# Group norms whose sums of squares are taken two products of z later, in a fused decoder step

## The chip, the cores and the metric

The kernel runs on one core of a Trainium2 chip. The metric is the device time of one execution in microseconds (us); lower is better. The engines are named as the profile names them: PE (TensorE matmul), DVE (VectorE), ACT (ScalarE), POOL (GpSimd) and SP (SyncE, which only issues DMAs here).

## What is computed

One inference step of a two-layer decoder for 1024 new prompt tokens and 8 short sample sequences (1104 token columns in all): a layer with a Mamba-2 mixer and an MLP, and a layer with attention and an MLP. The change lies in the first layer's mixer, between the state-space scan and the residual stream. What the scan gives, y, is gated by z, normed in 8 groups of 256 features, and projected:

```python
def gated_group_rmsnorm(y, z, w):
    g = (y * jax.nn.silu(z)).astype(jnp.float32)
    shp = g.shape
    g = g.reshape(shp[:-1] + (N_GROUPS, shp[-1] // N_GROUPS))
    g = g * lax.rsqrt(jnp.mean(g * g, axis=-1, keepdims=True) + EPS)
    return (g.reshape(shp) * w.astype(jnp.float32)).astype(y.dtype)
...
    y, h_new = ssd_scan(xs, dt, a_neg, bm, cm, h0)
...
    out = gated_group_rmsnorm(y, z, gate_w) @ w_out
```

z is the part of the input projection, `rmsnorm(h) @ w_in`, with 2048 columns: 8 groups of 256.

## The kernel before

Everything is kept with features in partitions and tokens along the free axis. Every fp32 product is three matmuls of split operands (`mm3`, L204 to L206: high weight by high data, high by low, low by high).

**The scan.** `ssd` (L609) runs group by group, in each group first a step for the sample tokens (t = 8) and then eight steps of 128 tokens. The step for the samples multiplies the states h by their decay on POOL (L716, four times), adds the new part in four pieces on DVE (L725, each from a pair of matmuls L723 and L724), and forms outputs (L679, L688). The prompt's steps form the next state from a state product (L729) and an addition (L734).

**The gate groups.** `gate_group` (L739) does for one group and each of three chunks of tokens (384, 384, 336) two products of z, one per tile of 128 features, of 24 matmuls each. After each, ACT takes tanh (L753) and DVE forms silu (L754). Then POOL multiplies y in (L759), ACT squares (L760), DVE adds the two tiles (L761) and `rstd` gives the scale: `sum_over` splits the sum into a high part (ACT, L248, `msh`) and a low part (DVE, L249, `msl`), PE multiplies both by ones (L250, L253), and ACT takes Ln (L261) and Exp (L262), each with a load of its function table. DVE multiplies scale and weight into the result (L765, twice). At the end of groups 0 to 5 `side_sums` (L776) stores sums of blocks of the result to DRAM (`z_d`); groups 6 and 7 are stored as they are (`g_d`, L774). The buffer that holds silu and squares comes from a ring of two tiles (`n3`), so chunk c + 2 waits for the last use in chunk c.

The function is a generator. Group 0 is mixed into the scan's last group: the table in `mixer` tells how many of its steps are taken after which scan step. Groups 1 to 7 run back to back in `gates_out` (L799).

**The output product.** `block_products` (L1182) multiplies with a scheme of seven block products instead of eight, in two blocks b, four output tiles p, seven products i. A block product is 18 matmuls of 276 columns. Its operands are seven slots, each loaded from `z_d` (L1174) and split by ACT (L1178) and DVE (L1179): for b = 0 a tile `A5`, two in `R0`, and four pieces of the buffer `S` that held the normed input of the z products, so these four can be loaded only when the last z product is done. Their splits are made in `more`, after products 1 to 4 of the first output tile. The weights of an output tile p are two raw tiles (L1113), of which DVE forms sums (L1119, L1125) and ACT and POOL the split parts (L1000, L1001). Raw tiles of odd p are taken from the ring `n3` that the norm also uses. Results are added by DVE (L1213), the first copied by ACT (L1232). PE's result banks are named `ma` to `md`.

The order on each engine is set by a scheduler when the program is built: it takes the earliest instruction in program order that its own timeline has ready, so code order sets priority and not place. `keep_in_program_order` on an instruction (argument `pin` of `sum_over`) keeps it from being taken before what stands ahead of it.

Of the kernel before, what the change touches and what calls it, by code (L numbers as in the profile page):

```python
# [16 lines left out]
P = 128  # L17
# [124 lines left out]
class Kernel:  # L142
# [96 lines left out]
    def sum_over(self, ssum, n, pin=False):  # L239


        nc = self.nc
        if self.pstat is None:
            ms = self.gps()
        else:
            ms = self.pstat[0].tile([P, 512], F32, tag=self.pstat[1], bufs=self.pstat[2], name="ms")
# [492 lines left out]
    def gate_group(self, g, xs, y, gt, tmp):  # L739
# [6 lines left out]
        for c, (o, n) in enumerate(CH):  # L746
            yv = [t[:, o:o + n] for t in y]
            g2 = gt(c)[:, :, :n]
            for j in range(2):
                pt = self.gps()  # L750
                self.mm3(pt[:, :n], [(w[j][0][:, k], w[j][1][:, k]) for k in range(KT)],
                         [(xs[c][0][:, k, :n], xs[c][1][:, k, :n]) for k in range(KT)])
                nc.scalar.activation(out=g2[:, j], in_=pt[:, :n], func=AF.Tanh, scale=0.5)  # L753
                nc.vector.scalar_tensor_tensor(out=g2[:, j], in0=g2[:, j], scalar=1.0, in1=pt[:, :n],  # L754
                                               op0=ALU.add, op1=ALU.mult)
                yield
# [5 lines left out]
            rs = self.rstd(g2[:, 0], n, self.eps4, D / 256, g2[:, 1])  # L762
            for j in range(2):
                ft = 2 * g + j
                nc.vector.scalar_tensor_tensor(out=yv[j], in0=yv[j],  # L765
                                               scalar=self.nv[:, ft % 8, 6 + ft // 8:7 + ft // 8], in1=rs,
                                               op0=ALU.mult, op1=ALU.mult)
            yield
        if g < 2 * KB:
# [29 lines left out]
    def gates_out(self, xs, big, cr, co):  # L799
# [3 lines left out]
        self.more_banks(cr, 4)  # L803
# [10 lines left out]
        slots = [[A5] + B + S[:4], [S[4], None, A5] + S[:4]]  # L814
        load, parts = self.side_io(self.rz, slots)
        with ExitStack() as cy:
            yp = self.pool("yp", ctx=cy)
            for g in range(1, G):
                y = yp.tile([P, 2, T], F32, tag="y", bufs=2, name="gy")
                for _ in self.gate_group(g, xs, [y[:, 0], y[:, 1]], lambda c: self.n3(),  # L820
                                         lambda: yp.tile([P, nn], F32, tag="m", bufs=2, name="gm")):
                    pass
                self.split_ahead()
                if g == 4:
                    for i in range(3):
                        load(0, i)
                if g in (5, 6):
                    for i in ((0,), (1, 2))[g - 5]:
                        parts(0, i)
# [3 lines left out]
        dp = self.pool("dp", ctx=co)  # L833
        us = dp.tile([P, 4, nn], F32, name="us")
        slots[1][1] = dp.tile(slot, F32R, name="A6")
# [296 lines left out]
    def down_blocks(self, layer, rd, rt, R0, big, c0, chs):  # L1132
# [12 lines left out]
        slots = [A, B + A[:5], A[5:] + B + A[:3], A[3:] + A[:3]]  # L1145
# [24 lines left out]
    def side_io(self, rt, slots):  # L1170
        nc = self.nc

        def load(b, i):
            nc.sync.dma_start(out=slots[b][i][:, 1].bitcast(F32), in_=rt[b][:, i // 2, i % 2])  # L1174

        def parts(b, i):
            x = slots[b][i]
            nc.scalar.copy(out=x[:, 0], in_=x[:, 1].bitcast(F32))  # L1178
            nc.vector.tensor_tensor(out=x[:, 1], in0=x[:, 1].bitcast(F32), in1=x[:, 0].bitcast(F32), op=ALU.subtract)  # L1179
        return load, parts  # L1180

    def block_products(self, w, big, us, slots, load, parts, free, make, last, more, early=(0, 0)):  # L1182
# [31 lines left out]
        for b in range(nb):  # L1214
            for p in range(4):
# [3 lines left out]
                for i, (wh, wl) in enumerate(self.down_weights(w[b], p)):  # L1219
# [4 lines left out]
                    x = slots[b][i]  # L1224
                    for k in range(2):
                        cs = slice(k * qw, k * qw + qw)
                        self.mm3(banks[e][:, 512 + (k - 1) * qw:512 + k * qw], [(wh[:, q], wl[:, q]) for q in range(KB)],
                                 [(x[:, 0, q, cs], x[:, 1, q, cs]) for q in range(KB)], new)
# [503 lines left out]
    def first_layer(self, cb):  # L1732
# [6 lines left out]
        with ExitStack() as ch:  # L1739
            cr = ExitStack()  # L1740
            self.banks(cr, 3)
            with ExitStack() as cm:
                self.fmp = self.pool("fmp", ctx=cm, right=True)
                self.cw = self.pool("cw", ctx=cm, right=True)
                with ExitStack() as c1:
                    xs = self.mixer(c1)
            big = self.pool("hp", ctx=ch, right=True).tile([P, KT, T], F32, name="hh")
            hts = [big[:, :, o:o + n] for o, n in CH]
            done, norm = self.entry(big, h_d, self.ncol(2))
            with ExitStack() as self.cR:  # L1750
                with ExitStack() as co:
                    self.gates_out(xs, big, cr, co)
# [94 lines left out]
    def mixer(self, c1):  # L1847
# [36 lines left out]
        for g in range(G):  # L1884
# [7 lines left out]
            for t in self.ssd(g, fm):  # L1892
                for k in range({8: 3, 2: 1, 3: 1, 4: 1, 6: 1, 7: 1}.get(t, 0) if gate is not None else 0):
# [75 lines left out]
```

## Time and profile before

| | |
|---|---|
| runs shown, us | 2946.33, 2947.52, 2948.03 (median 2947.52) |
| the profiled execution, us | 2948.11 |
| its span in the trace, us | 2946.4 |
| mean granted clock of PE | 0.985 |
| busy: PE, DVE, ACT, POOL | 96%, 64%, 49%, 47% |
| share of the chain that ended last: PE, DVE, issue, ACT, DMA, POOL | 72%, 9%, 6%, 5%, 5%, 4% |

The span is the stretch from the first to the last recorded instruction. A timeline row has the start in us, the length in us, the engine, the line and the operation, then result and operands, and in brackets the idle time of that engine ahead of it and what ended it. Starts of matmuls are a better guide than their lengths, since they are pipelined.

### The profile page before, as it was taken

What the parts mean: (1) busy time and instruction counts of PE and PEld (TensorE: products, weight loads), DVE (VectorE), ACT (ScalarE), POOL (GpSimd) and SP (SyncE); (2) the same over time, 40 slices, a digit from 0 to 9 for tenths busy, and PEclk for the clock granted to TensorE, in tenths of its full rate; (3) what the DMA queues carried; (4) which work ended last, traced back from release to release, by engine and by line L of the source; (5) the groups of instructions that cost most, each with busy time, mean ns of one, the idle gap of its engine ahead of it and who ended that gap; (6) DMA issues with size and microseconds to landing.
All of it is one profiled execution on the core that took longest, in us unless ns stands there. A gap on an engine that the chain in (4) does not pass through costs nothing.

```text
span 2946.4 us, 51820 instructions
## 1 busy us (share of the span) xinstructions
PE 2819.3 (96%) x19895; PEld 2710.3 (92%) x19895; DVE 1894.1 (64%) x3026; ACT 1454.8 (49%) x2781; POOL 1381.2 (47%) x1279
## 2 busy tenths in 40 slices
PE   8999999989878999999999999999999999999998
PEld 6999999978878999999999999988889999999997
DVE  6788777765546666454546766675678554367675
ACT  6555555556665355545433425555555545433333
POOL 5566666665445714444346663312112444345562
PEclk9999999999999999999999999999999999999999
DMA  3344444447554233444645522447454444543422
GB/s 136 95 125 128 123 122 124 129 136 268 186 196 142 87 113 117 151 140 150 245 159 190 183 80 69 160 155 266 143 177 171 140 147 135 203 151 123 144 99 76
DMA packets 219329, 433.46 MB, mean 147 GB/s; under 512 B 30713, under 2 KB 128377, under 8 KB 216505
## 3 DMA queue, kind: packets, MB, share of 16 engines
q1 hardware_dynamic: 219080, 430.14, 44.3%
q8 instruction: 157, 2.57, 0.4%
q14 instruction: 92, 0.75, 0.1%
HBM read 302.71 MB, written 128.32 MB: 146 GB/s over the span
## 4 chain that ended last, share of the span: by engine, by line
PE 72%; DVE 9%; issue 6%; ACT 5%; DMA 5%; POOL 4%; SPq 0%; DVEq 0%; POOLq 0%; ACTq 0%
PE g L204 9%; PE g L205 9%; PE g L206 9%; PE mc L204 3%; PE mc L206 3%; PE mc L205 3%; PE ma L204 3%; PE ma L206 3%; PE ma L205 3%; PE md L205 2%; PE md L206 2%; PE mb L204 2%; PE mb L205 2%; PE mb L206 2%; PE md L204 2%
## 5 line engine op out<-in xcount | busy, mean ns | idle before, releaser
L1001 POOL TENSOR_TENSOR w<-s,w 128x384 fp32r<-128x384 f32 (+1 forms) x272 | 369.6, 1364 | 394.1 <-ACT w L1000 390.0
L204 PE MATMUL g<-S,w 128*128 128x384 f32 (+2 forms) x1584 | 536.0, 339 | 2.4 <-ACT w L170 0.8
L205 PE MATMUL g<-S,w 128*128 128x384 f32 (+2 forms) x1584 | 536.3, 339 | 0.0
L206 PE MATMUL g<-S,w 128*128 128x384 f32 (+2 forms) x1584 | 532.9, 337 | 3.5 <-POOL w L171 2.7
L1001 POOL TENSOR_TENSOR w<-raw,w 128x384 fp32r<-128x384 f32 (+1 forms) x204 | 263.7, 1298 | 283.6 <-ACT w L1000 250.5
L171 POOL TENSOR_TENSOR w<-raw,w 128x1024 fp32r<-128x1024 f32 x96 | 244.1, 2543 | 274.9 <-ACT w L170 201.9
L206 PEld LDWEIGHTS g<-S,w 128*128 128x128 f32 x1584 | 304.1, 192 | 5.4 <-POOL w L171 3.0
L204 PEld LDWEIGHTS g<-S,w 128*128 128x128 f32 x1584 | 303.1, 191 | 5.9 <-issue 1.8
L205 PEld LDWEIGHTS g<-S,w 128*128 128x128 f32 x1584 | 303.7, 192 | 1.0 <-issue 0.5
L1000 ACT CAST w<-s 128x384 fp32r<-128x384 f32 (+1 forms) x272 | 150.0, 557 | 298.5 <-DVE s L1125 70.8
L204 PE MATMUL ma<-S,w 128*128 128x276 f32 (+1 forms) x808 | 235.2, 291 | 8.2 <-DVE us L1213 6.7
L206 PE MATMUL ma<-S,w 128*128 128x276 f32 (+1 forms) x808 | 234.5, 290 | 0.0
L205 PE MATMUL ma<-S,w 128*128 128x276 f32 (+1 forms) x808 | 234.3, 290 | 0.0
L1000 ACT CAST w<-raw 128x384 fp32r<-128x384 f32 (+1 forms) x204 | 112.2, 556 | 166.3 <-PE mc L206 49.1
L593 DVE SCALAR_TENSOR_TENSOR fm<-xp,cv,fm 128x1024 f32<-128x1024 f32 x96 | 161.1, 1681 | 33.1 <-ACT fm L574 32.5
L204 PEld LDWEIGHTS ma<-S,w 128*128 128x128 f32 x808 | 153.2, 190 | 9.9 <-issue 5.6
L205 PE MATMUL g<-R,w 128*128 128x384 f32 (+2 forms) x480 | 158.1, 329 | 0.0
L206 PE MATMUL g<-R,w 128*128 128x384 f32 (+2 forms) x480 | 157.9, 329 | 0.0
L204 PE MATMUL g<-R,w 128*128 128x384 f32 (+2 forms) x480 | 157.7, 329 | 0.0
L205 PEld LDWEIGHTS ma<-S,w 128*128 128x128 f32 x808 | 153.5, 190 | 0.0
L206 PEld LDWEIGHTS ma<-S,w 128*128 128x128 f32 x808 | 153.3, 190 | 0.0
L204 PE MATMUL mc<-S,w 128*128 128x276 f32 (+1 forms) x512 | 148.4, 290 | 1.9 <-DVE hh L1213 1.9
(489 smaller groups left out, 8671.1 us busy)
## 6 DMA issues: line engine op xcount, KB each, us to landing
raw<-in_w_up_dram SPq DMA_DIRECT2D x64, 512.0 KB
raw<-in_w_in_dram SPq DMA_DIRECT2D x48, 512.0 KB
raw<-in_w_downs_dram SPq DMA_DIRECT2D x64, 384.0 KB
w<-ws_o SPq DMA_DIRECT2D x48, 512.0 KB
w<-ws_q SPq DMA_DIRECT2D x40, 512.0 KB
ab<-acs_d SPq DMA_DIRECT2D x64, 256.0 KB
S<-t_d SPq DMA_DIRECT2D x18, 828.0 KB
S<-t_e SPq DMA_DIRECT2D x18, 816.0 KB
```

Of the source, the lines that this page charges most:

```text
L171: nc.gpsimd.tensor_tensor(out=wl, in0=raw, in1=wh.bitcast(F32), op=ALU.subtract)
L204: mm(out=out, lhsT=wh, rhs=xh, start=(first and k == 0), stop=False)
L205: mm(out=out, lhsT=wh, rhs=xl, start=False, stop=False)
L206: mm(out=out, lhsT=wl, rhs=xh, start=False, stop=(k == n - 1))
L593: nc.vector.scalar_tensor_tensor(out=acc[:, :SEQ], in0=xp[:, k:k + SEQ], scalar=cv[:, j, k:k + 1], in1=acc[:, :SEQ], op0=ALU.mult, op1=ALU ...
L1000: nc.scalar.copy(out=t[:, 0], in_=src)
L1001: nc.gpsimd.tensor_tensor(out=t[:, 1], in0=src, in1=t[:, 0].bitcast(F32), op=ALU.subtract)
```

## The change

`gate_group` no longer ends a chunk with its norm. It gives control back twice per chunk instead of three times, and puts the norm (the new `gate_norm`) into a list with a count of 3; `tick`, called once per product of z, counts down and runs what is due, so a norm is written two products behind its chunk, with its first ones-matmul pinned. Group 0's table of steps has one entry less. Group 1 begins, with two chunks, before the next buffers are opened. The last two chunks' norms would have no products of z behind them: they are run from `more`, after the first output tile's products 3 and 6, with their sums in a bank of the output product. To let the last group's y live that long its pools are laid out anew: the two y tiles come from pools of their own, and the operand `A6` is made of a rest of `S` and of a y tile, so slots are lists of pieces.

```diff
@@ gate_group
                 nc.vector.scalar_tensor_tensor(out=g2[:, j], in0=g2[:, j], scalar=1.0, in1=pt[:, :n],
                                                op0=ALU.add, op1=ALU.mult)
-                yield
+                if j == 0:
+                    self.tick()
+                    yield
...
             nc.vector.tensor_tensor(out=g2[:, 0], in0=g2[:, 0], in1=g2[:, 1], op=ALU.add)
-            rs = self.rstd(g2[:, 0], n, self.eps4, D / 256, g2[:, 1])
-            for j in range(2):
-                ft = 2 * g + j
-                nc.vector.scalar_tensor_tensor(out=yv[j], in0=yv[j],
...
+            self.due.append([3, partial(self.gate_norm, g, c, y, g2, tmp)])
+            self.tick()
             yield
+
+    def tick(self, n=1):
+
+        for e in self.due:
+            e[0] -= n
+        while self.due and self.due[0][0] <= 0:
+            self.due.pop(0)[1]()
+
+    def gate_norm(self, g, c, y, g2, tmp):
+        nc = self.nc
+        o, n = CH[c]
+        rs = self.rstd(g2[:, 0], n, self.eps4, D / 256, g2[:, 1], pin=True)
+        for j in range(2):
+            ft = 2 * g + j
+            yv = y[j][:, o:o + n]
+            nc.vector.scalar_tensor_tensor(out=yv, in0=yv, scalar=self.nv[:, ft % 8, 6 + ft // 8:7 + ft // 8], in1=rs,
+                                           op0=ALU.mult, op1=ALU.mult)
+        if c < 2:
+            return
@@ gates_out
-        slots = [[A5] + B + S[:4], [S[4], None, A5] + S[:4]]
+        slots = [[[(t[:, 0], t[:, 1])] for t in ts] for ts in ([A5] + B + S[:4], [S[4], A5, A5] + S[:4])]
...
+        for g in range(1, G):
+            for _ in gate if g == 1 else self.gate_of(g, xs, yps):
+                pass
...
         def more(b, p, i):
-            if (b, p) == (0, 0) and 1 <= i <= 4:
+            if (b, p) != (0, 0):
+                return
+            if 1 <= i <= 4:
                 parts(0, i + 2)
+            if i in (3, 6):
+
+                self.pstat = (self.pq, self.CHAIN[0][3], 1, 1024)
+                self.tick(2 if i == 3 else 9)
+                self.pstat = None
+            if i == 6:
+
+                t = ya.tile([P, 4, nn], F32R, tag="y", bufs=1, name="A6")
+                rest = self.S.rearrange("p e k n -> p (e k n)")[:, 5 * size:].rearrange("p (q n) -> p q n", q=2)
+                slots[1][1] = [(rest, t[:, 0:2]), (t[:, 2:3], t[:, 3:4])]
...
-                            (lambda: self.block_load(rd, 3, R0), lambda j: self.block_parts(j, R0)), more, (0, 1))
+                            (lambda: self.block_load(rd, 3, R0), lambda j: self.block_parts(j, R0)), more, (1, 1))
@@ side_io, parts
-            x = slots[b][i]
-            nc.scalar.copy(out=x[:, 0], in_=x[:, 1].bitcast(F32))
-            nc.vector.tensor_tensor(out=x[:, 1], in0=x[:, 1].bitcast(F32), in1=x[:, 0].bitcast(F32), op=ALU.subtract)
+            for hi, lo in slots[b][i]:
+                nc.scalar.copy(out=hi, in_=lo.bitcast(F32))
+                nc.vector.tensor_tensor(out=lo, in0=lo.bitcast(F32), in1=hi.bitcast(F32), op=ALU.subtract)
@@ first_layer
+                gate = self.gate_of(1, xs, yps)
+                for _ in range(4):
+                    next(gate)
             big = self.pool("hp", ctx=ch, right=True).tile([P, KT, T], F32, name="hh")
@@ mixer
-                for k in range({8: 3, 2: 1, 3: 1, 4: 1, 6: 1, 7: 1}.get(t, 0) if gate is not None else 0):
+                for k in range({8: 2, 2: 1, 3: 1, 6: 1, 7: 1}.get(t, 0) if gate is not None else 0):
```

What this moves is shown at three places by the written order of the engines; the changed program has its own line numbers (a norm's multiplies are L783 there, L765 before; the h additions L726 and L725; ones-matmuls L251, L254 and L250, L253; operand casts L1212 and L1178; weight loads L1143 and L1113).

DVE in the scan's last group, from the first to the fourth addition to the states h, before:

```order
L725 TENSOR_TENSOR h_7085<-h_7085,st 128x512
L679 TENSOR_TENSOR yo<-y,ef 128x256
L765 SCALAR_TENSOR_TENSOR gy<-gy,nv,gt 128x384 x2
L688 SCALAR_TENSOR_TENSOR yt<-fm,dcol,y 128x128 x2
L632 TENSOR_TENSOR xdt<-tp,dt 128x256
L725 TENSOR_TENSOR h_7085<-h_7085,st 128x512
L649 TENSOR_TENSOR dec<-dec,cbm 128x512
L641 TENSOR_TENSOR cbm<-cb,tri 128x128
L725 TENSOR_TENSOR h_7085<-h_7085,st 128x512
```

and now:

```order
L726 TENSOR_TENSOR h_7085<-h_7085,st 128x512
L680 TENSOR_TENSOR yo<-y,ef 128x256
L689 SCALAR_TENSOR_TENSOR yt<-fm,dcol,y 128x128 x2
L633 TENSOR_TENSOR xdt<-tp,dt 128x256
L726 TENSOR_TENSOR h_7085<-h_7085,st 128x512
L650 TENSOR_TENSOR dec<-dec,cbm 128x512
L633 TENSOR_TENSOR xdt<-tp,dt 128x256
L642 TENSOR_TENSOR cbm<-cb,tri 128x128
L726 TENSOR_TENSOR h_7085<-h_7085,st 128x512
```

The two multiplies of group 0's first norm stood between the first and the second addition; now they stand 33 rows behind the second.

PE at the end of the last product of z, before (`ma<-A` is the output product's first):

```order
L206 MATMUL g<-S,w 128x336
L250 MATMUL ms<-msh,ones_r 128x384
L253 MATMUL ms<-msl,ones_r 128x384
L250 MATMUL ms<-msh,ones_r 128x336
L253 MATMUL ms<-msl,ones_r 128x336
L204 MATMUL ma<-A_7815,w 128x276
```

and now, at the same place and where the last sum went:

```order
L206 MATMUL g<-S,w 128x336
L251 MATMUL ms<-msh,ones_r 128x384
L254 MATMUL ms<-msl,ones_r 128x384
L204 MATMUL ma<-A_7967,w 128x276
...
L206 MATMUL md<-S,w 128x276
L251 MATMUL ms<-msh,ones_r 128x336
L254 MATMUL ms<-msl,ones_r 128x336
L205 MATMUL mc<-S,w 128x276
```

Chunk 1's sums stay in front of the output product; chunk 2's stand behind its first six products, ahead of all but one matmul of the seventh.

ACT behind the last product of z now, from chunk 1's Ln to chunk 2's high part (`n_9421` is chunk 1's buffer, `n_9492` chunk 2's):

```order
L262 ACT_TABLE_LOAD
L262 ACTIVATE n_9421<-ms,eps 128x384
L1030 CAST w<-raw 128x384 x2
L763 ACTIVATE n_9492<-gy 128x336
L1212 CAST S<-S 128x1656
L263 ACT_TABLE_LOAD
L263 ACTIVATE n_9421<-n_9421 128x384
L763 ACTIVATE n_9492<-gy 128x336
L1212 CAST S<-S 128x1656
L1266 COPY us<-ma 128x552
L1212 CAST S<-S 128x1656
L249 CAST msh<-n_9492 128x336
```

Two more casts of `S` follow, one cast of a weight sum and one of a raw weight, and then the Ln and Exp of chunk 2, each with its table load. Before, chunk 1's Ln and Exp stood ahead of the first cast, chunk 2's Ln and Exp among the last two.

## Rows read from the trace of the kernel before

**Rows 1.** Busy time by stage: stretch, length, busy us of PE, PEld, DVE, ACT, POOL, granted clock, DMA

```profile
606.00:635.05 29.05, 23.41 (x155) 20.09 (x154) 18.49 (x39) 16.38 (x39) 17.27 (x18) 0.88 0.38 94
635.05:668.00 32.95, 30.49 (x204) 26.64 (x205) 23.30 (x52) 18.88 (x43) 25.34 (x27) 1.00 0.64 199
668.00:876.00 208.00, 181.96 (x999) 175.46 (x998) 109.09 (x148) 136.35 (x197) 96.07 (x62) 0.95 0.58 206
876.00:892.25 16.25, 2.47 (x4) 1.31 (x5) 11.23 (x15) 11.90 (x17) 3.10 (x3) 0.56 0.66 267
895.01:905.90 10.89, 8.64 (x64) 7.97 (x63) 8.24 (x9) 7.41 (x11) 8.29 (x7) 1.00 0.46 149
905.90:917.20 11.30, 11.30 (x89) 11.30 (x90) 8.63 (x11) 4.45 (x7) 6.05 (x6) 1.00 0.79 274
```

**Rows 2.** What PE waited for, 668 to 870 us: total us, times, longest

```profile
PE ms L253 <- DVE msl L249: 14.8, 8, 3.0
PE ms L250 <- ACT msh L248: 9.6, 8, 2.6
```

**Rows 3.** Timeline of ACT, end of the scan

```profile
624.64 1.28 ACT L261 ACT_TABLE_LOAD   x1 [4.48 <-PE g L253]
```

**Rows 4.** Timeline of DVE, end of the scan: the additions to the states h

```profile
621.46 0.69 DVE L725 TENSOR_TENSOR h<-h,st 128x512 f32<-128x512 f32 x1 [1.40 <-POOL h L716]
...
630.30 0.68 DVE L725 TENSOR_TENSOR h<-h,st 128x512 f32<-128x512 f32 x1
...
634.22 0.68 DVE L725 TENSOR_TENSOR h<-h,st 128x512 f32<-128x512 f32 x1
```

**Rows 5.** Timeline of PE, the first prompt step's state product

```profile
635.05 0.67 PE L729 MATMUL st<-xd,Bt 128*128 128x256 f32 x2 [0.50 <-DVE h L725]
```

**Rows 6.** Timeline of POOL, the states' decay

```profile
616.30 5.12 POOL L716 TENSOR_TENSOR h<-h,eendb 128x512 f32<-128x512 f32 x4
```

**Rows 7.** Busy time of the block products' tile `ma` in two stretches, PE first

```profile
892.25:895.01 2.76, 2.76 (x12) 2.76 (x13) 0.00 (x0) 0.00 (x0) 0.50 0.00 0
906.97:909.26 2.29, 2.29 (x18) 2.23 (x18) 0.00 (x0) 0.00 (x0) 1.00 1.09 332
```

**Rows 8.** Timeline of PE, end of the gate groups and output product

```profile
880.00 0.69 PE L250 MATMUL ms<-msh,ones_r 128*128 128x384 f32 x1 [4.03 <-ACT msh L248]
881.26 0.69 PE L253 MATMUL ms<-msl,ones_r 128*128 128x384 f32 x1 [0.57 <-DVE msl L249]
890.09 0.65 PE L250 MATMUL ms<-msh,ones_r 128*128 128x336 f32 x1 [8.15 <-ACT msh L248]
891.80 0.65 PE L253 MATMUL ms<-msl,ones_r 128*128 128x336 f32 x1 [1.06 <-DVE msl L249]
...
917.06 0.29 PE L206 MATMUL mb<-R,w 128*128 128x276 f32 x1
```

**Rows 9.** Timeline of ACT, end of the gate groups

```profile
882.03 1.28 ACT L261 ACT_TABLE_LOAD   x1 [0.38 <-PE ms L253]
883.32 0.58 ACT L261 ACTIVATE n<-ms,eps 128x384 f32<-128x384 f32 x1
...
885.64 1.55 ACT L1178 CAST S<-S 128x1656 fp32r<-128x1656 f32 x1
...
889.57 0.47 ACT L248 CAST msh<-n 128x336 fp32r<-128x336 f32 x1 [0.52 <-DVE n L761]
```

**Rows 10.** Timeline of DVE, start of the output product

```profile
899.20 1.03 DVE L765 SCALAR_TENSOR_TENSOR gy<-gy,nv,n 128x336 f32<-128x336 f32 x2
900.16 1.87 DVE L1179 TENSOR_TENSOR S<-S 128x1656 fp32r<-128x1656 f32 x1
...
905.51 0.69 DVE L1119 TENSOR_TENSOR s<-raw 128x384 f32<-128x384 f32 x1 [2.00 <-DMA raw<-in_w_outs_dram]
```

**Rows 11.** DMA issues of SP, start of the output product

```profile
899.79 0.80 SPq L774 DMA_DIRECT2D g_d<-gy  x2
900.68 0.81 SPq L1113 DMA_DIRECT2D raw<-in_w_outs_dram  x1
```

More of the change, by code (lines that the diff above doesn't have):

```diff
@@ L245, in sum_over @@
         else:
[L246 removed]
+            ms = self.pstat[0].tile([P, self.pstat[3] if len(self.pstat) > 3 else 512], F32, tag=self.pstat[1],
+                                    bufs=self.pstat[2], name="ms")
         hi, lo = (self.np.tile([P, 384], F32R, tag="n1", bufs=5, name="ms" + p)[:, :n] for p in "hl")
@@ L797, in side_sums, with gate_of, gates_out @@
             nc.sync.dma_start(out=d[:, 2, 1, cs], in_=t)
-    def gates_out(self, xs, big, cr, co):
+    def gate_of(self, g, xs, yps):
+        y = yps[g % 2].tile([P, 2, T], F32, tag="y", bufs=1, name="gy")
+        return self.gate_group(g, xs, [y[:, 0], y[:, 1]], lambda c: self.n3(),
+                               lambda: yps[0].tile([P, T // 2], F32, tag="m", bufs=2, name="gm"))
+    def gates_out(self, xs, big, cr, co, cb, yps, gate):
         nc = self.nc
         nn = T // 2
-        self.more_banks(cr, 4)
+        ya = yps[1]
         for c, (o, n) in enumerate(CH):
@@ L813, in gates_out @@
         B = cut(R0.rearrange("p e k n -> p (e k n)"), 2)
-        slots = [[A5] + B + S[:4], [S[4], None, A5] + S[:4]]
+        slots = [[[(t[:, 0], t[:, 1])] for t in ts] for ts in ([A5] + B + S[:4], [S[4], A5, A5] + S[:4])]
         load, parts = self.side_io(self.rz, slots)
[L816 to L829, printed above, removed]
+        for g in range(1, G):
+            for _ in gate if g == 1 else self.gate_of(g, xs, yps):
+                pass
+            self.split_ahead()
+            if g == 4:
+                for i in range(3):
+                    load(0, i)
+            if g in (5, 6):
+                for i in ((0,), (1, 2))[g - 5]:
+                    parts(0, i)
         cr.close()
@@ L1144, in down_blocks @@
         B = cut(R0.rearrange("p e k n -> p (e k n)"), 2)
-        slots = [A, B + A[:5], A[5:] + B + A[:3], A[3:] + A[:3]]
+        slots = [[[(t[:, 0], t[:, 1])] for t in ts] for ts in (A, B + A[:5], A[5:] + B + A[:3], A[3:] + A[:3])]
         free = [(0, 1, 2, 3, 4), (0, 1, 2, 3, 4), (0, 1, 4, 5, 6)]
@@ L1173, in load @@
         def load(b, i):
-            nc.sync.dma_start(out=slots[b][i][:, 1].bitcast(F32), in_=rt[b][:, i // 2, i % 2])
+            q = 0
+            for hi, lo in slots[b][i]:
+                m = lo.shape[1]
+                nc.sync.dma_start(out=lo.bitcast(F32), in_=rt[b][:, i // 2, i % 2, q:q + m])
+                q += m
         def parts(b, i):
-            x = slots[b][i]
-            nc.scalar.copy(out=x[:, 0], in_=x[:, 1].bitcast(F32))
-            nc.vector.tensor_tensor(out=x[:, 1], in0=x[:, 1].bitcast(F32), in1=x[:, 0].bitcast(F32), op=ALU.subtract)
+            for hi, lo in slots[b][i]:
+                nc.scalar.copy(out=hi, in_=lo.bitcast(F32))
+                nc.vector.tensor_tensor(out=lo, in0=lo.bitcast(F32), in1=hi.bitcast(F32), op=ALU.subtract)
         return load, parts
@@ L1223, in block_products @@
                         banks[e] = self.pq.tile([P, 1024], F32, tag=e, bufs=1, name="m" + e)
-                    x = slots[b][i]
+                    x = [(hi[:, q], lo[:, q]) for hi, lo in slots[b][i] for q in range(lo.shape[1])]
                     for k in range(2):
@@ L1227, in block_products @@
                         self.mm3(banks[e][:, 512 + (k - 1) * qw:512 + k * qw], [(wh[:, q], wl[:, q]) for q in range(KB)],
-                                 [(x[:, 0, q, cs], x[:, 1, q, cs]) for q in range(KB)], new)
+                                 [(hi[:, cs], lo[:, cs]) for hi, lo in x], new)
                     pv = banks[e][:, 512 - qw:512 + qw]
@@ L1750, in first_layer @@
             with ExitStack() as self.cR:
-                with ExitStack() as co:
-                    self.gates_out(xs, big, cr, co)
+                with co:
+                    self.gates_out(xs, big, cr, co, cz, yps, gate)
                 self.out_last(hts, done, norm)
```

13 lines of the change are left out of this document (7 added, 6 removed).

## The prediction

> **What bounds the kernel now.** I read the busy shares first, then TensorE's (PE's) busy time stage by stage, then the list of what PE waited for, and last the timelines around the places that the change moves. PE is busy 96% of the span, so time can only be won where PE idles or runs at its lower clock (a granted clock of 0.50, 1.2 GHz, against 1.00, 2.4 GHz). The stage table [rows 1] shows that in the part that the change touches. In 606 to 635 us (end of the state-space scan, with gate group 0 mixed in) PE is busy 23.41 of 29.05 us at a mean granted clock of 0.88. In 668 to 876 (gate groups 1 to 7) it idles 26.0 us in 16 or more short waits. In 876 to 892.25 (the last group's norm) it works 2.47 of 16.25 us, and in 895 to 905.9 it idles 2.25 us more. After 905.9 it never idles. These are the three places: start, middle, end.
>
> **The middle: 0, bounds -2 and +2.** The waits there are all for the operands of the ones-matmuls that add up a group's squares: 14.8 us for the low part on VectorE (DVE), 9.6 us for the high part on ScalarE (ACT) [rows 2]. One reads the change as pushing these sums back behind two more products of z, which would remove all of it. But the written order of PE differs there by three matmuls at most in group 1 and not at all in groups 2 to 6: the scheduler had already put each sum some 40 to 90 matmuls (two to four products) behind the product that feeds it, and the pin fixes what was there. ACT's and DVE's orders agree as well. So the 24 us of waits stay; I allow 2 us either way for shifted buffers and transfers.
>
> **The start: -4.5, bounds -7.5 and +1.** Before, chunk 0's norm stands among the last scan steps. ACT reaches its Ln at 624.64, after waiting 4.48 us for PE's low sum [rows 3]; DVE's four additions to the state h stand around the two multiplies of that norm, and run from 621.46 to 634.90, the second only at 630.30 [rows 4]. The first state product of the prompt's steps then starts at 635.05, after a wait of 0.50 for the last h addition [rows 5]. In the change no norm stands between these additions (the order of DVE above), and the 24 z products that PE ran between the two sums come earlier, where it idled. How early can that state product be? By DVE: POOL's four multiplies on h run 616.30 to 621.42 [rows 6]; after them four additions of 0.69 with a matmul pair of some 0.7 between them take 4 x 0.69 + 4 x 0.7 = 5.6, so 627.5 to 628 if POOL starts them a little later. By PE's own work: 29.05 - 23.41 = 5.64 us of idle go at most, and if all the time at half clock goes too (a mean of 0.88 is 24% of 29 us, 7.0 us, in which it did what takes 7.0 x 0.127 / 0.230 = 3.9 us at full clock by [rows 7]) another 3.1, so not before 626.3. The ceiling is therefore 635.05 - 627.5 = 7.5 us. The other end: the norm isn't gone. Two table loads, Ln, Exp, and the DVE multiplies move to the next steps, of 33 us in which PE already idles 2.46 us [rows 1], and three norms are in work there instead of two; a step held up by them costs about the 0.5 us of such a wait today [rows 5], so losing everything and two waits more is +1. I take -4.5: the ceiling less some 3 us for the six or so scan steps that now have no z product to fill their waits of 0.5 us each.
>
> **The end: +2.6, bounds -8 and +11.** Before, the four ones-matmuls of the last two chunks stand in front of the output projection's first product: PE waits 4.03 us, 0.57, then 8.15 for chunk 2's high part and 1.06 for its low part [rows 8], and the first block product starts at 892.25. In the change chunk 1's two sums still stand there, while chunk 2's stand 109 matmuls later. The new times, step by step. (1) Chunk 1's sums end about where they did, at 880 to 882 (PE waits 3.2 us for them instead of 4.03, since chunk 0's Ln and Exp stand in another place of ACT's list), so block products start there, 10 to 12 us earlier than at 892.25. (2) Three of them have their operands by then, loaded and split during groups 4 to 6: 3 x 2.29 = 6.9 us [rows 7], to about 887. (3) The other four need tiles that ACT casts in 1.55 us [rows 9] and DVE reduces in 1.87 [rows 10]. ACT's list in the change (above) puts a table load, Ln, two casts of weights and a square, 1.28 + 0.58 + 1.0 + 0.5, before the first of these casts, which starts at about 886.7, and table load, Exp and a square between first and second. With ACT never idle, casts end at 888.2, 892.4, 895 and 898 and the low parts at 890.1, 894.3, 896.9 and 899.8. PE waits 3.1, then 1.9, then 3.1 us for them. (4) Chunk 2's sums come at about 902.4, the seven block products end at 904.6, about 8 us earlier than before. (5) Now the weights of the second product, p = 1. Half of that raw block lies in the buffer of the norm, which comes free with chunk 2's last multiply. Before, that multiply ran at 899.20 [rows 10]; the stores followed at 899.79, the load at 900.68 [rows 11], and DVE, idle for 2.00 us on that transfer alone, read it at 905.51 [rows 10]: 4.8 us from issue to use, just in time. In the change the norm follows the sums at 902.4: 2 x 1.28 + 0.58 + 0.5 plus 0.5 for its place in ACT's list, and two multiplies of 1.0 in all, so 907.2. Store and issue take it to 907.8, landing to 912.5, DVE's sum, ACT's cast and POOL's low part to 914.6. p = 1 has one block product that does not need it, done at 906.9, so PE waits 7.7 us. The second ends at 914.6 + 2.3 = 916.9; before it ended at 917.19 [rows 8]. **The gain of 12 us at the front is thus given back at the weight block: -0.3.** Counted by idle time it is much the same: 3.2 + 3.1 + 1.9 + 3.1 + 7.7 = 19.0 us against 13.8 + 2.25 = 16.0, less 2.4 us for sums and 12 products that ran at half clock before (those 12 took 2.76 us, at 0.230 each against 0.127 [rows 7]); that gives +0.6, and I keep -0.3.
>
> One price is left, the clock. Gaps of about 3 us have a price behind them here: the stage of 208 us has a mean of 0.95 [rows 1], so 20.8 us at half clock for 16 waits, 1.3 us each. Work at half clock loses 1 - 0.127 / 0.230 = 45%, 0.58 us a gap, 2.9 us for five. Its bounds are 0 and 5 x 18 x 0.103 = 9.3 us, a whole block product of 18 matmuls after each gap. -0.3 + 2.9 = +2.6. The bounds of the whole term: -8 if the weight block is in time and no clock is lost, +11 if the chain behind the operands is slow (+8.1 on top, below).
>
> Splitting one operand into two pieces adds one DMA, one cast and one subtraction of the same bytes, beside PE and after 907. A one-bank-wider sum tile costs nothing on any engine; it uses a bank that block products fill later.
>
> **Sum.** -4.5 + 0 + 2.6 = -1.9 on the profiled execution's 2948.11 us, which is 0.59 above the runs' median of 2947.52: **2945.6 us** on the median's basis. A measurement of this kernel can tell about 0.2%, 5.9 us, from no change; this is inside it.
>
> **A rule beside the trace.** On ACT a table load lasts 1.28 us, and the activation behind it starts 0.01 us after its end (882.03 + 1.28, then 883.32) [rows 9], so I price a switch at 1.28. The Trainium skill (ScalarE: Activation LUTs, What ACT_TABLE_LOAD costs) has about 1.38 us of drain on top, 2.66 us a switch. By that, chunk 2's norm, which has two switches on the chain to the weight block, would be 2.8 us later and the sum +0.9, at 2948.4; the trace speaks against it.
>
> **Rivals.**
> *Faster: the weight block is in time.* The 7.7 us wait of p = 1 is a chain of seven links worked out by hand; if ACT reaches chunk 2's cast and Ln 5 us or more sooner, or the block lands during other work, it goes, with 0.6 us of clock: 2.6 - 8.3 = -5.7, and with the start -10.2: **2937.3**. For it: ACT's list holds some 14 us of work from chunk 1's Ln to the last operand cast, and what of it starts sooner than worked out here counts in full. Against it: the chain is serial and four casts of 1.55 stand in it.
> *Slower: the same weight block, later still.* Place: from the operands' casts to chunk 2's multiply to the load. Before, the five operands took from 885.64 on ACT [rows 9] to 902.03 on DVE [rows 10], 16.4 us; at that pace from 886.7 they end at 903.1 and not 899.8, 3.3 later. And the load is issued with two stores and the next operands' loads around it; if it takes twice 4.8, that is 4.8 more. +8.1: **2953.7**. It decides from a last multiply after about 910 or a landing after 918. Against it: before, ACT also waited in that stretch for the sums of chunk 2 (0.52 at 889.57 [rows 9]), which now stand behind the casts.
> *The page's rule:* 2948.4, as above.
> That the change doesn't do what it says is true of the middle, by the order, and is in the forecast: were it false and the sums' waits gone, 24 us would go; the two orders are alike, so I give it no share of its own.
>
> **How the numbers follow.** Forecast, between 2941.6 and 2950: 0.44. Faster rival 0.28, slower rival 0.17, the page's rule 0.05, something not seen (schedule shifts in later layers, where the order differs by a few rows) 0.06. Faster by over 0.2%: 0.28 + 0.03 = 0.31. Within: 0.44 + 0.05 + 0.01 = 0.50. Slower: 0.17 + 0.02 = 0.19. The range takes in both rivals' times and the bounds of the start: 2936 to 2955; forecast and page's rule alone would have 2941 to 2951.
>
> **What would show it.** Right: the waits of 668 to 876 unchanged near 24 us for the sums' operands; the first prompt state product 4 to 7 us earlier; block products from about 880; a PE gap of several us in p = 1, ended by a weight that DVE started after a DMA wait. Wrong: sums' waits gone in the middle; no such gap in p = 1 (faster), or one over 12 us (slower); the start no earlier.

## The result: slower by 0.37%, outside the range

The changed kernel takes 2958.1 us (median of 6 runs, 2954.68 to 2959.67) against 2947.12 us (6 runs, 2944.76 to 2948.03); the ratio is 1.0037, 95% interval 1.0024 to 1.005. The forecast was 2945.6, the range ended at 2955.

Where do the 11 us lie? Both programs issue the same 19,895 matmuls, so one can ask in each trace when PE reaches the same count. Four stretches hold nearly all of it. They run from the 3,900th matmul to the 4,215th (the end of the scan, called *start* below), from there to the last product of z (*groups*), from there to the 5,700th (the *end* of the prediction: last norm and first output tiles), and, where nobody had looked, from the 14,900th to the 15,200th, where the second layer's up projection begins (*second layer*).

The busy time in these stretches, for the kernel before (length, busy us of PE, PEld, DVE, ACT, POOL, granted clock, share of DMA, GB/s):

```profile
605.41:660.07 54.66, 46.56 (x320) 39.21 (x317) 38.19 (x87) 33.03 (x77) 37.08 (x42) 0.94 0.47 129
660.07:875.96 215.89, 189.89 (x1044) 183.39 (x1043) 113.26 (x152) 138.90 (x202) 102.19 (x66) 0.95 0.60 210
875.96:952.27 76.31, 60.24 (x443) 58.41 (x443) 47.37 (x58) 37.65 (x57) 38.43 (x31) 0.89 0.44 156
2264.22:2306.44 42.22, 39.31 (x301) 38.42 (x301) 31.84 (x32) 24.53 (x38) 24.65 (x16) 1.00 0.50 172
```

And the same for the changed kernel:

```profile
605.36:663.91 58.55, 47.40 (x321) 39.39 (x318) 37.07 (x87) 31.14 (x75) 39.50 (x44) 0.91 0.48 131
663.91:877.59 213.68, 190.35 (x1044) 184.07 (x1043) 110.85 (x153) 140.91 (x203) 98.01 (x64) 0.94 0.58 209
877.59:957.71 80.12, 64.31 (x442) 62.77 (x443) 46.25 (x58) 37.30 (x58) 35.48 (x30) 0.87 0.42 148
2269.35:2317.84 48.49, 42.29 (x302) 41.32 (x301) 33.63 (x33) 24.69 (x38) 25.30 (x16) 0.93 0.44 149
```

Start +3.9, groups -2.2, end +3.8, second layer +6.3: 11.8 us, of 11.1 between the spans (2957.5 and 2946.4). In the third row PE's busy time for the same matmuls is longer (64.31 against 60.24): it worked 13.9 us of it at half clock, and 5.3 us before.

**The start.** The first state product of the prompt's steps starts at 630.56, where it was 635.05 [rows 5]. Then ACT stops. Its timeline in the changed kernel:

```profile
623.46 1.28 ACT L647 ACTIVATE dec<-ab,acs 128x128 f32<-128x128 f32 x4 [0.46 <-PE y L656]
...
631.75 1.28 ACT L647 ACTIVATE dec<-ab,acs 128x128 f32<-128x128 f32 x4 [2.94 <-DMA ab<-acs_d]
632.94 0.84 ACT L754 ACTIVATE gt<-g 128x384 f32<-128x384 f32 x2
633.68 0.62 ACT L649 ACTIVATE dec<-dec 128x512 f32<-128x512 f32 x1
634.20 0.25 ACT L636 COPY Bt<-tp 128x128 f32<-128x128 f32 x1
```

SP's issues, and PE behind ACT's copy:

```profile
625.22 0.55 SPq L693 DMA_DIRECT2D y_d<-yt  x1
625.88 1.58 SPq L624 DMA_DIRECT2D ef<-eacs_d  x2
627.55 0.55 SPq L620 DMA_DIRECT2D ab<-acs_d  x1
628.20 0.55 SPq L693 DMA_DIRECT2D y_d<-yt  x1
628.84 4.58 SPq L620 DMA_DIRECT2D ab<-acs_d  x2
```

```profile
634.50 0.47 PE L628 MATMUL tp<-ident,fm 128*128 128x128 f32 x1 [3.05 <-ACT Bt L636]
```

Each scan step loads decay rows (`ab`) into a ring of two buffers, so the load for one step can be issued only when the step two before has been read. That was done at 624.74 (623.46 + 1.28). The load went out at 627.55, because a store and two loads stood ahead of it in SP's queue, and it was used at 631.75, 4.2 us later. The faster steps reach ACT before it is there. The copy that PE needs stands behind that wait in ACT's queue. PE idles 3.05 us, the clock is at half from 633.17 to 640.00, and most of the gain is gone: counted from the 3,900th matmul, the changed kernel is 4.9 us ahead at the 4,050th and 0.5 us at the 4,200th.

The +3.9 at the end of the stretch comes from the next wait, for the sum of group 0's chunk 1. The kernel before makes a wait of this kind later, 2.97 us for the low part of a sum of group 1. The two rows, the changed kernel first:

```profile
661.50 0.69 PE L251 MATMUL g<-msh,ones_r 128*128 128x384 f32 x1 [2.15 <-ACT msh L249]
```

```profile
681.84 0.45 PE L253 MATMUL ms<-msl,ones_r 128*128 128x384 f32 x1 [2.97 <-DVE msl L249]
```

With both the clock falls to half, from 660.48 to 667.31 here and from 683.40 to 686.82 before. The difference is +5.4 us at the 4,300th matmul and +0.7 at the 4,350th. So the border at the 4,215th matmul puts time into the start that the groups give back, and the -2.2 of the groups is no gain of theirs: start and groups are best read together, +1.7.

**The end** has the wait that was worked out. PE, ACT, DVE and SP in the changed kernel, for the second output tile's weights:

```profile
917.55 0.60 PE L204 MATMUL mb<-R,w 128*128 128x276 f32 x1 [7.82 <-ACT w L1030]
```

```profile
905.34 1.28 ACT L262 ACT_TABLE_LOAD   x1 [5.61 <-PE ms L254]
906.64 0.54 ACT L262 ACTIVATE n<-ms,eps 128x336 f32<-128x336 f32 x1
907.20 1.28 ACT L263 ACT_TABLE_LOAD   x1
...
916.99 0.98 ACT L1030 CAST w<-s 128x384 fp32r<-128x384 f32 x2 [6.60 <-DVE s L1149]
```

```profile
909.08 1.05 DVE L783 SCALAR_TENSOR_TENSOR gy<-gy,nv,n 128x336 f32<-128x336 f32 x2 [3.35 <-ACT n L263]
...
916.39 1.03 DVE L1149 TENSOR_TENSOR s<-raw 128x384 f32<-128x384 f32 x2 [5.63 <-DMA raw<-in_w_outs_dram]
```

```profile
909.67 0.81 SPq L792 DMA_DIRECT2D g_d<-gy  x2
910.57 0.81 SPq L1143 DMA_DIRECT2D raw<-in_w_outs_dram  x1
```

Read against [rows 10, 11]: the last norm's multiply came at 899.20 and now at 909.08, the load behind it at 900.68 and now at 910.57, and DVE waited 2.00 us for it and now 5.63.

**The second layer.** No line of it was changed. DVE in the kernel before, where the up projection's second pair of weights begins:

```profile
2277.77 2.43 DVE L1099 TENSOR_TENSOR R<-R 128x1088 fp32r<-128x1088 f32 x1 [2.46 <-ACT R L1098]
2280.12 0.71 DVE L1030 TENSOR_TENSOR rx<-mc,rx 128x544 f32<-128x544 f32 x1
```

In the changed kernel:

```profile
2285.94 4.68 DVE L1129 TENSOR_TENSOR R<-R 128x1088 fp32r<-128x1088 f32 x2
2290.83 3.16 DVE L1040 TENSOR_TENSOR s<-raw 128x512 f32<-128x512 f32 x2 [0.21 <-DMA raw<-in_w_up_dram]
2293.91 0.71 DVE L1060 TENSOR_TENSOR rx<-mc,rx 128x544 f32<-128x544 f32 x1
```

What PE waited for in 2264 to 2310 us there (total us, times, longest):

```profile
PE md L204 <- ACT w L1030: 3.7, 1, 3.7
PE mc L204 <- DVE rx L1060: 2.4, 1, 2.4
```

The scheduler put DVE's instructions in another order. The addition that frees a result bank (`rx<-mc`) now stands behind two weight sums that read a transfer which had only just landed. Earlier in the stretch the first weight sums (`s<-raw`) stand behind both last subtractions of the operands (`S<-X,S`) and not between them. Before:

```profile
2269.10 1.29 DVE L1010 TENSOR_TENSOR s<-raw 128x512 f32<-128x512 f32 x2
2270.31 1.29 DVE L964 TENSOR_TENSOR S<-X,S 128x1088 fp32r<-128x1088 f32 x1
```

And in the changed kernel:

```profile
2274.10 2.48 DVE L994 TENSOR_TENSOR S<-X,S 128x1088 fp32r<-128x1088 f32 x2
2276.50 1.29 DVE L1040 TENSOR_TENSOR s<-raw 128x512 f32<-128x512 f32 x2
```

PE's waits are 6.1 us instead of 2.9, and 6.8 us run at half clock instead of none.

### The profile page after: what moved, and what is told of

It reads as the page before. It is cut to its first block, busy times and chain, and to the rows that moved or that the text cites. A ratio compares the mean times of both kernels' runs of the same rounds, so it can differ in the third digit from the quotient of the medians.

```text
span 2957.5 us, 51821 instructions
## 1 busy us (share of the span) xinstructions
PE 2829.4 (96%) x19895; PEld 2719.1 (92%) x19895; DVE 1888.0 (64%) x3027; ACT 1454.4 (49%) x2782; POOL 1370.7 (46%) x1279
## 4 chain that ended last, share of the span: by engine, by line
PE 59%; DVE 7%; ACT 4%; issue 4%; DMA 3%; POOL 3%; SPq 0%; DVEq 0%; ACTq 0%; POOLq 0%
PE g L204 6%; PE g L206 6%; PE g L205 6%; PE mc L204 4%; PE mc L205 3%; PE mc L206 3%; PE ma L204 3%; PE ma L205 3%; PE ma L206 3%; PE md L206 3%; PE md L205 3%; PE mb L204 3%; PE mb L206 3%; PE md L204 3%; PE mb L205 3%
```

## The experiments

The theory from here on: three separate causes. (1) The start's gain is lost to the load of `ab`. (2) The end loses to the weight block of p = 1. (3) The second layer loses by a changed order that comes with the changed start. The rivals stand in the expectations. All variants are edits of the changed kernel unless they say otherwise. The lengths of the four stretches, in us, from the busy-time view of each profile, and the ratios to the kernel before from the timed runs:

| kernel | start | groups | end | second layer | ratio, 95% interval |
|---|---|---|---|---|---|
| before | 54.7 | 215.9 | 76.3 | 42.2 | 1 |
| the change | 58.6 | 213.7 | 80.1 | 48.5 | 1.0037 (1.0024 to 1.005) |
| end_only | 54.1 | 209.4 | 79.8 | 43.3 | 0.9998 (0.9989 to 1.0007) |
| start_only | 58.1 | 212.5 | 76.7 | 46.7 | 1.0029 (1.0019 to 1.0038) |
| none | 53.9 | 209.9 | 75.6 | 43.3 | 0.998 (0.997 to 0.9989) |
| wring | 57.4 | 212.9 | 69.7 | 43.8 | 0.9986 (0.9976 to 0.9995) |
| ab3 | 52.5 | 213.6 | 79.3 | 48.4 | 1.0019 (1.001 to 1.0028) |
| after_rxfirst | 57.5 | 213.2 | 79.2 | 45.5 | 1.0032 (1.0019 to 1.0044) |
| before_farpin | 54.8 | 216.0 | 76.3 | 44.8 | one run |
| end_wring | 54.8 | 209.0 | 69.7 | 43.3 | 0.996 (0.9945 to 0.9975) |
| end_wring2 | 54.3 | 209.3 | 70.5 | 41.9 | 0.9962 (0.9949 to 0.9974) |
| wring_ab3 | 52.2 | 211.5 | 69.8 | 44.2 | 0.9968 (0.9956 to 0.9979) |
| combo | 52.5 | 212.6 | 69.9 | 45.8 | 0.9978 (0.9969 to 0.9987) |

The lengths are of one profiled execution each. How far they vary is seen in end_wring and end_wring2, which are the same program: by 0.5, 0.3, 0.8 and 1.4 us. In the second layer PE's waits are the same in both (1.5, 0.7 and 0.5 us), but in one the clock is at half for 3.4 us and in the other not at all. A difference of 1.5 us between two rows therefore says little.

### One part at a time

**end_only**: only the last chunk's norm is late. Group 0 gives control back three times per chunk again, and group 1 no longer begins ahead of the next buffers.

```diff
-                if j == 0:
+                if j == 0 or g == 0:
...
-            self.due.append([3, partial(self.gate_norm, g, c, y, g2, tmp)])
+            if (g, c) == (G - 1, 2):
+                self.due.append([3, partial(self.gate_norm, g, c, y, g2, tmp)])
+            else:
+                self.tick(99)
+                self.gate_norm(g, c, y, g2, tmp, False)
...
-                for _ in range(4):
-                    next(gate)
...
-                for k in range({8: 2, 2: 1, 3: 1, 6: 1, 7: 1}.get(t, 0) if gate is not None else 0):
+                for k in range({8: 3, 2: 1, 3: 1, 4: 1, 6: 1, 7: 1}.get(t, 0) if gate is not None else 0):
```

> The changed kernel with only the last chunk's norm moved into the output product; all other norms and group 0's table of steps as before. Theory (two separate causes): the end alone costs 3.3 us (a PE wait of about 7.8 us for p = 1's weights, and half clock behind it), and the 6.5 us lost in the second layer come from the start, since this program's order there is that of the kernel before: 2947.1 + 3.3 = 2950.4, and the PE stretch from the 14,900th to the 15,200th matmul takes 42.2 us as before. Rival (the second layer's loss follows from the end, or is chance): that stretch takes 48.5 us and the time is about 2957.

Measured: 2946.99 us, ratio 0.9998. The end costs 3.5 us, as in the whole change, and the second layer takes 43.3 us, so the end alone does not bring its loss. But the total is below the expectation by 3 us: the groups take 209.4 us and not 215.9, though no norm is moved there. The theory had not foreseen that (see *none*).

**start_only**: the last group's norms at once, the rest as changed (`if g < G - 1:` in place of the condition above; the changed table and group 1's early begin stay).

> The changed kernel with the last group's norms made at once, in front of the output product, as before; the start and groups 1 to 6 as changed. Theory: the start gives nothing by the end of the gate groups (+0.7, +1.6 with the middle) and the second layer loses 6.5 us, since its order there is nearly that of the changed kernel: 2947.1 + 1.6 + 6.5 = 2955, with PE's waits at the end 13.8 us as before. Rival (all comes from the end): 2947 to 2949 and 42.2 us for the 14,900th to the 15,200th matmul.

Measured: 2955.86 us, ratio 1.0029. Start +3.4 us, end +0.4, second layer +4.5, so most of the second layer's loss comes without the end's change. PE's largest waits there, in 2266 to 2314 us:

```profile
PE md L204 <- ACT w L1034: 3.1, 1, 3.1
PE ma L204 <- ACT rx L1090: 1.3, 1, 1.3
PE mc L204 <- DVE rx L1064: 0.8, 1, 0.8
```

In this program the result's addition stands between the two weight sums and not behind both; the wait for it is 0.8 us and not 2.4. That made the addition's place a suspect of its own.

**none**: the changed layout, no norm late (the condition is `False`, the rest as in end_only).

> The changed program's layout (pools for y, A6 in two pieces, loads of the next block one product later) with every norm made at once, none moved, and group 0's table as before. Theory: the run with the end alone was 6.8 us ahead of the kernel before at the end of the gate groups, though nothing there was moved; if that is the new layout's effect on the scheduler's order in groups 1 to 6, this program shows it too: -6 to -8 us at the 5,200th matmul, no change behind it (the four sums wait 13.8 us in front of the output product), total 2940 to 2943. Rival (it came with the moved norm): within 2 us of the kernel before at the 5,200th matmul, total 2946 to 2949.

Measured: 2942.82 us, ratio 0.998. The theory holds: the layout alone is worth some 6 us in the groups. PE's waits in 660 to 870 us:

```profile
PE ms L254 <- DVE msl L250: 12.4, 6, 4.6
PE ms L251 <- ACT msh L249: 9.1, 7, 2.1
```

against 14.8 and 9.6 in [rows 2], a somewhat shorter stretch. PE's idle time in the groups is 21.5 us where it was 26.0. Some 3.4 us are won by the 4,350th matmul, past the place where the kernel before has its wait of 2.97 us at 681.84 with half clock behind it; from there the difference swings by several us until the 6 are left. So measured against its own layout, the change loses more than against the kernel before: the late norms, with group 1's early begin, cost 0.57% (1.0037 against 0.998). What in the layout makes the 6 us stays open, beyond that one wait. Every program with late norms of group 0 also begins group 1 early, so the runs do not tell which of the two takes part of the 6 us away.

### The end: where p = 1's weights lie

**wring**: in the first block of the output product p = 1 and p = 3 take their raw weights from the ring that p = 0 uses, and p = 2 takes the norm's.

```diff
-            t = self.np.tile([P, 2, KB, P], F32, tag="n3", bufs=2, name="raw") if p % 2 else self.raw([P, 2, KB, P])
+            t = self.np.tile([P, 2, KB, P], F32, tag="n3", bufs=2, name="raw") if (p == 2 if self.alt else p % 2) else self.raw([P, 2, KB, P])
...
+                self.alt = b == 0 and nb == 2
```

> The changed kernel, but in the output product's first block p = 1 takes its raw weights from the ring that p = 0 uses, and p = 2 from the norm's ring. Theory: p = 1's weights no longer wait for the last norm, PE's wait of 7.8 us ends and with it 10 us at half clock behind it (some 4 us): 2958.1 - 8 to - 12 = 2946 to 2950, with the second layer's 6.5 us still lost. Rival (p = 0's weights free that ring too late, so p = 1 waits as long): 2956 to 2958 and a wait of over 5 us in the first products of p = 1.

Measured: 2945.03 us, ratio 0.9986, 13 us below the change by the medians and 0.51%, 15 us, by the ratios. What PE waited for in 876 to 946 us, the three largest:

```profile
PE ms L251 <- ACT msh L249: 2.9, 1, 2.9
PE ma L205 <- DVE S L1213: 2.2, 1, 2.2
PE ma L204 <- DVE n L755: 0.9, 1, 0.9
```

The wait of 7.82 us is gone; the end takes 69.7 us, 6.6 less than before the change and 10.4 less than with it. One thing the expectation had wrong: the second layer lost 1.6 us here and not 6.5, since this program's order there has the addition ahead of the sums again. So of the 13 us some 4.7 belong there. The start is as changed here (57.4 us), so that loss does not follow from the changed start alone: an edit of a weight ring was enough to put the addition back.

**end_wring** and **end_wring2**: this edit with end_only's.

> Both edits: only the last chunk's norm is moved, and p = 1's raw weights come from the other ring. Theory: the end then gains 3.3 - 8 to - 12 = -5 to -9 us and the second layer loses nothing: 2938 to 2942, faster than both kernels. Rival (the end's gain is given back at the next wait, for p = 2's weights, which now take the norm's ring, or at half clock): 2945 to 2950.

> The kernel with only the last chunk's norm moved and p = 1's weights from the other ring, again, for a closer interval: ratio 0.9945 to 0.9975 if the first measurement stands, above 0.998 if it was chance.

Measured: 2936.87 and 2935.61 us, ratios 0.996 and 0.9962. This version beats both kernels, by 0.4% and by some 0.75%. Its 11 to 12 us are the layout's 6 to 7 in the groups and 6 to 7 at the end.

### The start: the third buffer

**ab3**: `tag="ab", bufs=2` becomes `bufs=3`, nothing else.

> The changed kernel with three buffers instead of two for the decay rows that each scan step loads (ab). Theory: the start's gain of 5 us was given back because ACT waited 2.94 us for such a load, issued only when a buffer came free; with a third buffer the load is a step earlier, that wait goes with the half clock behind it, and the 4,100th matmul comes 3 to 5 us earlier than in the kernel before instead of at the same time. What is left at the 4,400th: 0 to -4. Rival (the steps are bound by something else): 0 at the 4,100th matmul as in the changed kernel.

Measured: 2955.24 us, ratio 1.0019. The start's stretch:

```profile
608.23:660.69 52.46, 44.30 (x321) 36.33 (x317) 36.98 (x86) 30.55 (x74) 38.63 (x43) 1.00 0.50 138
```

52.5 us against 58.6 in the change and 54.7 before: no wait of ACT for `ab` is left, the granted clock is 1.00 in place of 0.91, and the 4,100th matmul comes 3.8 us earlier than before, counted from the 3,800th. At the 4,400th it is 6.9 us ahead, more than the 0 to 4 expected. The rival falls. By the ratios the third buffer is worth 0.18%, 5 us; the two intervals overlap a little, but with the weights mended (wring and wring_ab3 below) it is 0.18% again. That the ring's depth sets the wait is shown by this run. Whether two buffers would do if the load stood ahead of the store in SP's queue, no run shows. The second layer takes 48.4 us here, with the order of the change.

### The second layer: two rows of DVE's order

**after_rxfirst**: the next pair's weight sums are put behind the result's addition by an edge of order.

```diff
+            v = nc.vector.tensor_tensor(out=t, in0=a, in1=b, op=op)
+            if (layer, f) == (1, 3):
+                self.tc.add_manual_dep(v.ins, self.rx2.ins.name, mybir.DependencyInfo(
+                    mybir.DependencyClass.NoSync, mybir.DependencyReason.DATA), reason="keep_in_program_order")
...
+                v = tt(r[:, 3], pv, r[:, 3])
+                if (layer, f) == (1, 2):
+                    self.rx2 = v
```

> The changed kernel with one edge of order in the second layer: DVE adds the second product's result before it forms the next pair's weight sums, which read a late transfer; no other engine's order changes. Theory: the wait of 2.45 us for that result and the half clock behind it go, the stretch from the 14,900th to the 15,200th matmul takes 43.5 to 44.5 us and not 48.5, total 2953 to 2954. Rival (the loss is in the weights' first sums, which stand behind two subtractions, a wait of 3.67 us): the stretch stays over 47 us, total 2957 to 2959.

Measured: 45.5 us for the stretch, and 2957.64 us, ratio 1.0032. The wait for the addition went:

```profile
PE md L204 <- ACT w L1030: 3.7, 1, 3.7
PE ma L204 <- ACT rx L1093: 0.2, 1, 0.2
```

3.0 us of the 6.3 are this addition's place; the expectation (43.5 to 44.5) was too low, since the wait of 3.7 us that is left has 6.8 us at half clock behind it here. The stretch lies between theory and rival, the total where the rival had it: 1.0032 and 1.0037 overlap, so the timed runs alone do not tell the two kernels apart.

**before_farpin**: the kernel before, with the first weight sums pinned behind the operands' last subtractions.

```diff
+            a = nc.vector.tensor_tensor(out=lo, in0=src, in1=hi.bitcast(F32), op=ALU.subtract)
+            if temps is not None and i in (5, 6):
+                self.tc.keep_in_program_order(a)
...
+        a = nc.vector.tensor_tensor(out=s1, in0=a21, in1=a22, op=ALU.add)
+        if layer and not self.far:
+            self.far = 1
+            self.tc.keep_in_program_order(a)
```

> The kernel before with the second layer's first weight sums pinned behind the last two subtractions of the operands, as the changed kernel has them, but the result's addition ahead of the next pair's sums. Theory (the addition's place costs most): the stretch from the 14,900th to the 15,200th matmul takes 43.5 to 44 us against 42.2. Rival (the first sums' place costs most): 46 to 48.5 us.

Measured: 44.8 us, +2.6, between the two expectations. So the stretch's 6.3 us are two halves, 2.6 to 3.3 for the first sums' place and 3.0 for the addition's, each known to some 1.5 us. The one execution took 2959.05 us, but 8 us of that arose ahead of the stretch, in parts that the edit does not touch; the total is not read.

### All mended

**wring_ab3**: the whole change with both mends.

> The changed kernel with two mends: p = 1's raw weights from the other ring and a third buffer for the scan's decay rows. This program's order in the second layer also has the result's addition ahead of the next weight sums. Theory (the three named waits are the whole loss): against the kernel before, start -2.2 us (as with the third buffer alone), gate groups -2.5, end -6.6, second layer +1.6, together about -9.7: 2937 to 2940, ratio 0.996 to 0.998. Rival (the mends overlap, and a gain at the start is taken again at a wait behind it): as with the weights alone, ratio 0.9986, 2943 to 2946.

Measured: 2938.9 us, ratio 0.9968. The four stretches:

```profile
605.24:657.45 52.21, 44.13 (x320) 36.30 (x317) 37.31 (x86) 30.55 (x74) 39.16 (x43) 1.00 0.50 139
657.45:868.97 211.52, 188.80 (x1044) 183.37 (x1043) 110.43 (x153) 141.62 (x205) 98.83 (x66) 0.95 0.60 212
868.97:938.74 69.77, 62.18 (x442) 60.83 (x443) 44.77 (x57) 36.90 (x58) 34.75 (x30) 0.93 0.48 171
2252.05:2296.20 44.15, 41.45 (x302) 40.88 (x302) 32.22 (x31) 24.16 (x37) 25.71 (x16) 0.92 0.49 164
```

-2.5, -4.4, -6.5 and +1.9: the same change, with two waits taken out of its way, turns from 0.37% slower to 0.32% faster. Of the difference, 4.3 us lie in the second layer, whose order turned although neither mend aims at it.

**combo**: group 0's and the last chunk's norms late, the others at once, both mends and the addition first.

> Only group 0's norms and the last chunk's norm are moved, groups 1 to 6 make theirs at once; both mends, and the addition first in the second layer. Theory: start -2.2, gate groups -6 as where norms are made at once, end -6.6, second layer +3.3: about -11.5, 2935 to 2938, ratio 0.996. Rival (the gate groups' gain of 6 us hangs on group 0's order too): ratio 0.997 to 0.998.

Measured: 2942.23 us, ratio 0.9978. The total is the rival's. The groups take 212.6 us and not 209 to 210, so about half of their 6 us is lost though their own norms are made at once (the third buffer alone changed nothing there). That the loss comes from group 0's late norms is not shown: group 1's early begin is in this program too.

## Why the prediction was wrong

All four signs that the prediction named for being right came: the middle's waits, the earlier state product, block products from 882.51, the gap in p = 1. They tested the steps that it had priced, and what failed lay beside them.

**The middle** (0, bounds -2 and +2): measured -2.2, which the border of the stretches makes, and PE's waits for the sums' operands in 668 to 876 us are 23.2 us in all where they were 24.4 [rows 2]. That the waits stay was right. What it missed is that the new pools alone would have given 6 us there.

**The start** (-4.5, bounds -7.5 and +1) is the step of the sum that failed. Its first half came as forecast, 630.56 for the first state product against 635.05. The sentence that failed is "a step held up by them costs about the 0.5 us of such a wait today": the step was not held up by the norm but by its own load, which the prediction had not walked through SP's queue, and one wait of 3.05 us with half clock behind it took 4.4 us back. ab3 shows it: without that wait the start is 6.1 us shorter, 3.0 us of it idle time. The second wait, 2.15 us for chunk 1's sum from 659.35 on, falls on the border of the two stretches and is made up within some 25 us. Start and groups together came to +1.7 in place of -4.5.

**The end** (+2.6, bounds -8 and +11): measured +3.8. The mechanism was right, and that the sum came so near is luck in part. The wait of p = 1 was worked out at 7.7 us and is 7.82; both its ends came about 3 us later than worked out (909.73 and 917.55 against 906.9 and 914.6), 1.6 us of it because the groups ended later. The waits for the operands came to 3.9 us (0.36, 1.33 and 2.25) where 8.1 was put. So the idle time that the forecast counted, 19.0 us against 16.0, is 15.8, 0.3 us less than before. The clock made up for it: PE's busy time grew by 4.1 us, where the forecast has +0.5 (2.9 for the gaps less 2.4 for what had run at half clock before). The two misses, each over 3 us, cancel. Two steps do not add up as written: the terms from 882.03 put the first cast at 885.4 and not 886.7 (it came at 888.01), and those from 902.4 put the end of the last multiply at 907.5 and not 907.2. Neither decided anything. Of the last chunks only chunk 2's norm runs from `more`, after product 3 (of 0 to 6), and not both as the description of the change says: chunk 1's count runs out with the last product of z.

**The table loads**: the last norm's Ln starts 0.02 us after its table load ends (905.34 + 1.28, then 906.64), and the next load 0.02 us after that Ln ends (906.64 + 0.54, then 907.20). The rule in the Trainium skill (ScalarE: Activation LUTs, What ACT_TABLE_LOAD costs), with 1.38 us of drain on top, is not what this trace shows.

**What the sum left out**: the second layer's 6.3 us, put at nothing. The prediction had the changed rows of order there in view and gave them a chance of 0.06 and no price. Without them the result would have been about 2952, inside the range and still not the forecast. Of the 12.5 us between forecast and result, start and groups together make 6.2, the second layer 6.3 and the end 1.2 (the rest of the trace gives some of it back). The slower rival was a later weight block; the last multiply came at 909.08 and the block was read at 916.39, short of that rival's 910 and 918, so it was not the cause.

## What to carry to other kernels

A program whose order a scheduler sets can lose time 1,600 us away from an edit: read the new order of every engine to the end, and price each place where a row that frees a buffer falls behind a row that waits for a transfer. When steps get faster, walk the loads that feed them through their queue too; a ring of two buffers that was just deep enough becomes the next wait, the more so where stores stand ahead of its loads. A buffer shared by a norm and by weights ties the weights' transfer to the norm; before moving the norm later, move the weights to another ring.

## What was not expected

The cost of a short wait is more than the wait. Behind the 3.05 us at the scan's end PE ran 6.8 us at half clock, and the stretch that idles 3.0 us less than the change in ab3 is 6.1 us shorter. Yet such a price need not be paid each time: end_wring and end_wring2, one program, have the same waits in the second layer, and the clock fell in one of them only. Pools laid out anew, with one operand in two pieces and one load of the next block an output tile later, were worth 0.2% (ratio 0.998) with no norm moved; that is over half of what the change itself lost or, mended, won.
